# Gate projections by seven products ahead of the mLSTM, on normalised rows

## The chip, the cores and the metric

The kernel runs on one core of one Trainium2 chip. The metric is the device time of one execution in microseconds. Three runs of the kernel before gave 1904.54, 1907.61 and 1908.16 us: a median of 1907.61. The profile is one more execution, which took 1907.19 us.

## The reference

One layer of a hybrid encoder is applied to two request groups of 512 tokens each (x_prompt and x_sample, D = 1024), with shared weights:

```
u      = rmsnorm(x, g_mix) @ w_in       # one projection, its columns feed everything below
q, k   = silu(centred_conv(u[q,k], w))  # 4 heads of 128
v, o   = u[v], u[o]                     # 4 heads of 256 each; o gates the mLSTM's output
h      = mlstm(q, k, v, i, f), forward and backward, then a norm per head, times sigmoid(o)
a      = latent attention(cq, ckv, shared rotary key): 8 heads
y      = sigmoid(gm) * (h @ w_mo) + sigmoid(ga) * (a @ w_ao)
x      = x + y @ w_out
x      = x + swiglu(rmsnorm(x))         # the FFN
x      = x + gated embedding of p       # 256 -> 1024
out    = rmsnorm(x)
```

What matters here is that all columns of u come from the same normalised rows, and that o (8 blocks of 128 columns), gm and ga (8 blocks each) are plain 1024-to-128 projections, each behind a sigmoid.

## The kernel before

**Products.** Activations lie with features on the partitions and the 512 tokens of a group on the free axis. A product in fp32 is made of three matmuls of rounded parts, high by high, high by low and low by high. `proj1` (L173) does one block of 128 output columns for one group: 8 slices of the input times 3, so 24 matmuls of 128x512. `w8` (L186) loads a block of weights (512 KB) and splits it into `whi` (a cast on ScalarE) and `wlo` (a subtraction on VectorE).

**Seven products.** Some projections go by Strassen's scheme in Winograd's form. A quad is two output blocks by two input halves by two groups. `Ops` (L786) keeps the operands of the activation side: P1, P2 and P3 are plain quarters, P7, P6, P5 and Q4 are sums of them, and each is split into `xh` (ScalarE) and `xl` (VectorE). `Seven` (L847) loads four weight blocks, forms their sums on GpSimd and splits each into a high and a low half in one tile `wp` (L843 on ScalarE, L152 on VectorE); each product is 12 matmuls, so a quad takes 84 where eight products take 96. `chain` (L899) lets the products of neighbouring quads interleave, and `outputs` (L923) collects the banks: copies `u` on ScalarE, sums on VectorE. Before the change this serves the two branches' output projections ("mo", then "ao", whose operand sums are made by `oops`, L1013, on GpSimd except P7) and the FFN.

**The order of the work.** Everything below is told in the program's order; a scheduler moves instructions ahead where their inputs allow it.

- *Start.* x is loaded and multiplied by g_mix while it is split into `h` (pairs of high and low tiles of rows that are not yet normalised). `norm_x` (L292) squares x in place (six tiles on ScalarE, two on GpSimd), adds the squares (VectorE and GpSimd), and gets rstd per token from a matmul with ones (`sumsq`, into bank ssc) and one Newton sequence on VectorE (`rsqrt`). Since rows aren't normalised, each projection is multiplied by rstd on its way out of PSUM: `hproj` (L328) does it on VectorE for q, k, o and the merge gates; v has it as a scale. The latents (cq, ckv) and the mLSTM's gate logits are projected first.
- *Row computation.* The mLSTM's forget and input gates become cumulative rows on VectorE (L378 to L453, through two small transfers by way of DRAM); transposes on TensorE (`tpc`) turn them into columns `mcols`.
- *mLSTM.* `mlstm_proj(hd)` (L462) projects q, k, v and the two o blocks of a head. `mlstm_chain(hd, g)` (L531) does two passes for a group, one per direction: bc and bd (TensorE), exponentials into the tile `w` (ScalarE), a product with the scores (VectorE), `ph` (ScalarE) and `pl` (VectorE), then nm (TensorE, 128x258), the division and the norm, transposes `ht`, and `hz` (times the o gate). `w` has one buffer. The projections of head hd + 1 stand beside the chains of head hd.
- *The last head.* No projections are left for it. `lat_norms` (L608), which normalises the latents, stands ahead of the last head's chains, and ten merge gates (`merge_gate`, L642; `BULK[0] = 10`) beside them.
- *Attention*, with the other six merge gates between its heads, then the branches "mo" and "ao", the output projection, the embeddings (`emb`, L1102, whose weights sit in two of the tiles `wst` that `Seven` uses), the FFN, and the last norm.

Weights come by two queues, SP's and ScalarE's; SP's also carries stores of intermediate rows to DRAM (the merge gates to `tmd` and `tad`) and their loads.

## Time and profile before

| | |
|---|---|
| median of 3 runs | 1907.61 us (1904.54 to 1908.16) |
| the profiled execution | 1907.19 us, its span 1905.4 us |
| TensorE's granted clock, mean | 0.988 |
| busy: PE, DVE, ACT, POOL | 1849.6, 1242.5, 879.7, 477.5 us |
| DMA | 207.58 MB, mean 109 GB/s |

The profile's rows read as follows. In a timeline a row begins with its start and its duration in us, then engine, line, operation, result and inputs, tile sizes and a count; in brackets stands how long the engine had idled before, and what ended that. Matmuls overlap: one of 128x512 shows 0.39 us, but they start every 0.23 us, and it is the distance of starts that counts. In a table of stretches each engine has its busy time and, in brackets, its instructions; the number behind the engines is the clock that TensorE was granted, 1.00 being full. In a table of groups the time busy and the mean duration in ns stand behind the first bar, the idle time before such instructions behind the second. Stages by time in us, roughly: start 0 to 80, mLSTM heads 80 to 425, the last head's chains with ten merge gates 425 to 545, attention to 880, the branches to 1000, output projection and embeddings to 1150, the FFN to 1800, the end to 1905.

### The profile page before, as it was taken

The page shows a single profiled execution, that of the slowest core. Times are in us where ns is not written, and L with a number is a line of the kernel's source. Part 1 is how long each engine was busy: PE and PEld are TensorE (multiplying, and loading weights), DVE is VectorE, ACT ScalarE, POOL GpSimd, SP SyncE. Part 2 cuts the span into 40 slices and gives each one's busy share as a digit, 9 for nine tenths or more (in the row PEclk, how much of TensorE's full clock was granted, in tenths as well). Part 3 has the DMA queues.
Part 4 walks back from the last instruction along what each step waited for, and adds up shares of the span by engine and source line. Part 5 has one row for each costly group of instructions (what it writes and reads, how often), then busy time and mean ns, then how long its engine had stood idle before and what let it go on. Part 6 is the DMA issues. An engine that isn't in the chain of part 4 may idle for free.

```text
span 1905.4 us, 24519 instructions
## 1 busy us (share of the span) xinstructions
PE 1849.6 (97%) x8840; PEld 1538.6 (81%) x8840; DVE 1242.5 (65%) x2141; ACT 879.7 (46%) x1711; POOL 477.5 (25%) x346
## 2 busy tenths in 40 slices
PE   7999999999999999899989998999999999999997
PEld 6898998988888878677877886888888887888886
DVE  7657575836556567976897577444444558878757
ACT  5255555644444565784434354333333344434442
POOL 3000000100000000342550026666465652322100
PEclk9999999999999999999999998999999999999999
DMA  4111111122253123345455241233222346534242
GB/s 164 51 45 34 56 34 56 34 67 73 78 176 132 54 70 110 106 149 210 154 184 181 88 166 50 100 112 109 94 100 93 129 137 222 162 130 141 89 127 89
DMA packets 97881, 207.58 MB, mean 109 GB/s; under 512 B 10656, under 2 KB 21280, under 8 KB 97760
## 3 DMA queue, kind: packets, MB, share of 16 engines
q1 hardware_dynamic: 85664, 163.03, 25.5%
q10 hardware_dynamic: 12096, 43.00, 7.0%
q8 instruction: 69, 1.13, 0.2%
q14 instruction: 52, 0.43, 0.1%
HBM read 151.89 MB, written 54.10 MB: 108 GB/s over the span
## 4 chain that ended last, share of the span: by engine, by line
PE 85%; DVE 8%; issue 2%; ACT 2%; POOL 1%; DMA 1%; SPq 0%; DVEq 0%; ACTq 0%; POOLq 0%
PE b L894 12%; PE b L896 12%; PE b L895 12%; PE mm L183 8%; PE mm L181 8%; PE mm L182 8%; PE nm L580 3%; DVE xl L152 2%; PE mm L79 2%; PE mm L495 2%; PE mm L497 2%; PE mm L496 2%; PE pt L759 1%; DVE wp L152 1%; PE mm L1243 1%
## 5 line engine op out<-in xcount | busy, mean ns | idle before, releaser
L894 PE MATMUL b<-xh,wp 128*128 128x512 f32 x1148 | 444.1, 395 | 13.3 <-ACT wp L843 6.4
L895 PE MATMUL b<-xl,wp 128*128 128x512 f32 x1148 | 451.1, 393 | 4.9 <-DVE xl L152 4.9
L896 PE MATMUL b<-xh,wp 128*128 128x512 f32 x1148 | 447.2, 394 | 3.7 <-DVE wp L152 3.6
L843 ACT CAST wp<-wst 128x512 fp32r<-128x512 f32 (+1 forms) x271 | 164.7, 612 | 306.7 <-PE b L896 238.8
L152 DVE TENSOR_TENSOR wp<-wst,wp 128x512 fp32r<-128x512 f32 (+1 forms) x271 | 248.3, 918 | 76.7 <-ACT wp L843 76.1
L894 PEld LDWEIGHTS b<-xh,wp 128*128 128x128 f32 x1148 | 217.4, 189 | 66.4 <-ACT wp L843 8.8
L896 PEld LDWEIGHTS b<-xh,wp 128*128 128x128 f32 x1148 | 217.4, 189 | 53.5 <-DVE wp L152 6.0
L895 PEld LDWEIGHTS b<-xl,wp 128*128 128x128 f32 x1148 | 217.4, 189 | 52.1 <-DVE xl L152 5.3
L181 PE MATMUL mm<-hh,whi 128*128 128x512 f32 x592 | 233.7, 395 | 7.4 <-ACT whi L166 7.2
L183 PE MATMUL mm<-hh,wlo 128*128 128x512 f32 x592 | 233.1, 396 | 2.3 <-DVE wlo L152 2.2
L182 PE MATMUL mm<-hl,whi 128*128 128x512 f32 x592 | 233.4, 395 | 0.7 <-DVE hl L277 0.7
L869 POOL TENSOR_TENSOR s<-wst,wst 128x512 f32<-128x512 f32 (+1 forms) x42 | 75.6, 1800 | 432.8 <-DMA wst<-w 255.0
L934 DVE TENSOR_TENSOR u<-b,u 128x512 f32<-128x512 f32 x90 | 61.6, 689 | 141.4 <-PE b L896 85.3
L181 PEld LDWEIGHTS mm<-hh,whi 128*128 128x128 f32 x592 | 112.6, 190 | 31.2 <-ACT whi L166 7.2
L183 PEld LDWEIGHTS mm<-hh,wlo 128*128 128x128 f32 x592 | 112.4, 190 | 26.6 <-DVE wlo L152 3.4
L182 PEld LDWEIGHTS mm<-hl,whi 128*128 128x128 f32 x592 | 112.4, 190 | 24.5 <-DVE hl L277 1.3
L166 ACT CAST whi<-wst 128x1024 fp32r<-128x1024 f32 (+1 forms) x71 | 73.0, 1029 | 103.9 <-PE mm L182 63.4
L152 DVE TENSOR_TENSOR xl<-ld,xh 128x512 fp32r<-128x512 f32 x121 | 97.7, 837 | 11.6 <-ACT xh L1178 6.6
L152 DVE TENSOR_TENSOR wlo<-wst,whi 128x1024 fp32r<-128x1024 f32 (+1 forms) x71 | 86.7, 1221 | 25.1 <-ACT whi L166 24.8
L929 ACT COPY u<-b 128x512 f32<-128x512 f32 x90 | 50.9, 588 | 110.6 <-PE b L896 79.1
L152 POOL TENSOR_TENSOR vnl<-avt,vnh 128x512 fp32r<-128x512 f32 x16 | 21.4, 1337 | 283.6 <-ACT vnh L156 260.9
L495 PE MATMUL mm<-whi,hh 128*128 128x256 f32 x256 | 72.3, 283 | 0.2 <-DVE cu L329 0.2
(333 smaller groups left out, 3570.4 us busy)
## 6 DMA issues: line engine op xcount, KB each, us to landing
wst<-w SPq DMA_DIRECT2D x75, 512.0 KB
wst<-w ACTq DMA_DIRECT2D x60, 512.0 KB
ld<-actd SPq DMA_DIRECT2D x77, 256.0 KB
actd<-t SPq DMA_DIRECT2D x44, 256.0 KB
actd<-sg SPq DMA_DIRECT2D x33, 256.0 KB
x<-x SPq DMA_DIRECT2D x32, 256.0 KB
ld<-hzd SPq DMA_DIRECT2D x32, 256.0 KB
wst<-wd ACTq DMA_DIRECT2D x16, 512.0 KB
```

What stands on the lines that cost most here:

```text
L152: e.tensor_tensor(out=out, in0=src, in1=hi.bitcast(F32), op=ALU.subtract)
L166: S.copy(hi[:, :n], st[:, :n])
L181: E.matmul(bk, whi[:, c], hi, start=k == 0, stop=False)
L182: E.matmul(bk, whi[:, c], lo, start=False, stop=False)
L183: last_mm[0] = E.matmul(bk, wlo[:, c], hi, start=False, stop=k == nk - 1)
L495: E.matmul(out, hi[:, tb], whi[:, n], start=k == 0, stop=False)
L843: S.copy(hi, src)
L869: GP.tensor_tensor(out=src, in0=a11, in1=a21, op=ALU.add)
L894: E.matmul(bk, whi[:, c], hi, start=bool(first) and k == 0, stop=False, **sk)
L895: E.matmul(bk, whi[:, c], lo, start=False, stop=False, **sk)
L896: E.matmul(bk, wlo[:, c], hi, start=False, stop=k == self.kh - 1, **sk)
L934: V.tensor_tensor(out=t, in0=b, in1=t, op=ALU.add if name == "P2" else ALU.subtract)
```

## The change

The code of `Ops`, `Seven`, `chain` and `outputs` moves up unchanged but for a parameter that says where tiles lie. What it does:

- **Normalised rows.** x is no longer squared in place: ScalarE squares all tiles into other tiles, VectorE adds them in pairs, `sumsq` runs over four tiles of each group, rstd is spread by fp32 matmuls, and 16 VectorE instructions multiply x by g_mix and rstd in place.
- **Gates ahead.** On these rows 4 quads (the 8 o blocks) and 5 quads (10 of the 16 merge gate blocks) are done by seven products ahead of the mLSTM. Their tanh goes to DRAM (`tod`, `tmd`, `tad`), and the mLSTM loads its o gates from there. GpSimd makes their weight sums, VectorE their operand sums.
- **Behind that**, `h` is the normalised operands P1, P2, P3 and a split of the last quarter, so that q, k, v and the remaining merge gates need no multiplication by rstd: q and k are copied by ScalarE, the gates' tanh reads PSUM.
- **Pools.** The row computation's tiles are opened only once the chain's pools are closed, so it stands behind the chain.
- **The last head** has 2 merge gates beside it instead of 10; attention has 4 instead of 6.
- **Embeddings.** Their weights sit in four operand tiles of 128x512 instead of two of the `wst` tiles.
- **Second branch.** All operand sums of `oops` go to VectorE.

```diff
     def norm_x(g):
-        q = xs[g]
+        q = []
         for k in range(KD):
-            if k in (2, 5):
-                GP.tensor_tensor(out=q[k], in0=q[k], in1=q[k], op=ALU.mult)
-            else:
-                S.activation(out=q[k], in_=q[k], func=AF.Square)
-        for i, j, e in ((2, 5, GP), (0, 1, V), (3, 4, GP), (6, 7, V), (0, 3, V), (2, 6, V), (0, 2, V)):
-            e.tensor_tensor(out=q[i], in0=q[i], in1=q[j], op=ALU.add)
+            t = XT("t", "sq")
+            S.activation(out=t, in_=xs[g][k], func=AF.Square)
+            q.append(t)
+            if k % 2:
+                V.tensor_tensor(out=q[k - 1], in0=q[k - 1], in1=t, op=ALU.add)
+        pc = bank("ssc")
+        sumsq(pc, q[::2])
+        r = rsqrt(pc[:, 0 : 2 * NB], 2 * NB, 1.0 / D)
+        V.tensor_copy(out=rcol[g], in_=r)
+        bc = spread_f32(r)
         t = H("rs", "rs1")
-        S.copy(t, rstd_bank(q[:1], D, X0, rcol[g]))
+        S.copy(t, bc)
         rs1.append(t)
+        for k in range(KD):
+            x = xs[g][k]
+            V.scalar_tensor_tensor(out=x, in0=x, scalar=col("g_mix", k), in1=bc, op0=ALU.mult, op1=ALU.mult)
...
+    hx = Ops(lambda g, k: xs[g][k], lambda: XT("t", "t"), lambda n: V, place0)
+    hx.need("P7")
...
+    def first_pair(*cols_):
+        def put(at, t):
+            (kind, c), g = cols_[at[0]], at[1]
+            o = utile("o") if at == (0, 1) else t
+            S.activation(out=o, in_=t, func=AF.Tanh, scale=0.5)
+            if kind == "o":
+                S.activation(out=o, in_=o, func=AF.Identity, scale=hg[:, c : c + 1], bias=hg[:, c : c + 1])
+            nc.sync.dma_start(dsts[kind][g][c], o)
+
+        srcs = [a["w8"][W8[f"{kind}{c}"]] for kind, c in cols_]
+        return hx, lambda: Seven(srcs, 4, hx, outputs(put, utile))
...
+    quads = [first_pair(("o", 2 * i), ("o", 2 * i + 1)) for i in range(MH)]
+    quads += [first_pair(*bulk[2 * i : 2 * i + 2]) for i in range(FIRST)]
+    bulk = bulk[2 * FIRST :]
+    chain(quads, head=True)
...
+    h = [hx.x["P1"] + hx.x["P2"], bs + hx.x["P3"]]
+    WX.close()
+    XT.close()
+    MC = Slots("MC", sel=2)
+    R = Slots("R", "right", r=12, tr=2)
...
             for g in range(G):
-                bk = hproj(w, g, M1("tr", "cu"))
+                bk = M1("tr", "cu")
+                S.copy(bk, proj1(w, h[g]))
...
-        for c in range(2):
-            w = w8(f"o{2 * hd + c}")
-            for g in range(G):
-                to[g][c] = hproj(w, g, M1("to", "to"))
-                S.activation(out=to[g][c], in_=to[g][c], func=AF.Tanh, scale=0.5)
...
+        for g in range(G):
+            for c in range(2):
+                to[g][c] = M1("to", "to")
+                nc.sync.dma_start(to[g][c], tod[g][2 * hd + c])
...
             w = w8(f"{name}{c}")
             for g in range(G):
-            t = hproj(w, g, EV("bk", "tg"))
-            S.activation(out=t, in_=t, func=AF.Tanh, scale=0.5)
-            nc.sync.dma_start(dst[g][c], t)
...
+            t = EV("bk", "tg")
+            S.activation(out=t, in_=proj1(w, h[g]), func=AF.Tanh, scale=0.5)
+            nc.sync.dma_start(dsts[name][g][c], t)
...
-    oops = Ops(lambda g, k: load(ozd[g][k], X2, "x"), lambda: late["OP"]("ev", "t"), lambda n: V if n == "P7" else GP)
+    oops = Ops(lambda g, k: load(ozd[g][k], X2, "x"), lambda: late["OP"]("ev", "t"), lambda n: V)
...
-            st = [sl_("wst", "wst", F32, (P, 1024)) for sl_ in (WX, WX)]
-            for i in range(2):
-                nc.sync.dma_start(st[i], a["wple"][i])
+            st = [load(a["wple"][i // 2][:, i % 2 * T : i % 2 * T + T], OP, "ev") for i in range(4)]
...
-BULK = [10, 2, 1, 1, 0, 2, 0, 0, 0, 0]
+FIRST = 5
+BULK = [2, 1, 1, 1, 0, 1, 0, 0, 0, 0]
```

More of the change, by code (lines that the diff above doesn't have):

```diff
@@ L130, in bank @@
         return pb[0](n)
-    banks("P1", dict(mm=2, sc=2, tp=2, bc=2), mm="mm", sc="sT nm", tp="ssc tpc vtp ht", bc="bc bd rbc")
     cols = cp.tile([P, NCOL], F32, name="cols")
@@ new lines, in chain, with make @@
+    def chain(quads, head=False, look=4):
+        order = [(0, n) for n in ("P1", "P2", "P7")]
+        if head:
+            order = [(0, "P1"), (0, "P2"), (1, "P1"), (1, "P2"), (0, "P7"), (0, "P6"), (0, "P5"), (0, "Q4"), (1, "P7"), (0, "P3")]
+        for i in range(1 if head else 0, len(quads)):
+            for n in ("P6", "+P1", "P5", "+P2", "Q4", "+P7", "P3"):
+                if n[0] != "+":
+                    order.append((i, n))
+                elif i + 1 < len(quads):
+                    order.append((i + 1, n[1:]))
+        made = {}
+        def make(i):
+            if i not in made:
+                made[i] = quads[i][1]()
+        for at, (q, n) in enumerate(order):
+            for i, m in order[at : at + look + 1]:
+                quads[i][0].need(m)
+            for i, _ in order[at : at + 2]:
+                make(i)
+            made[q].product(n)
@@ L281, in encoder_kernel @@
     LAT = Slots("LAT", "right", raw=8)
     H = Slots("H", h=32, rs=2)
-    MC = Slots("MC", sel=2)
-    X0 = Slots("X0", x=16, raw=2, tr=15)
-    R = Slots("R", "right", r=12, tr=2)
+    XT = Slots("XT", x=16, t=28)
+    WX = Slots("WX", "right", wst=2, s3=2, wp=1)
+    banks("P0", dict(mm=4, tp=2, bc=2), mm="mm", tp="ssc", bc="rbc")
     h, rs1 = [], []
-    xs = [[X0("x", "x") for _ in range(KD)] for _ in range(G)]
+    xs = [[XT("x", "x") for _ in range(KD)] for _ in range(G)]
     def split_x(g):
@@ L316, in encoder_kernel @@
     split_x(0)
-    early["gate", 0] = raw(proj1(wg, h[0]), X0)
+    early["gate", 0] = raw(proj1(wg, h[0]), XT, "t")
     wq = w8("cq0")
```

313 lines of the change are left out of this document (153 added, 160 removed).

## The prediction

> **What bounds the kernel now.** I read the page first, then the busy time of each engine by stretches, then single rows. The page gives the span and TensorE's share.
>
> ```profile
> span 1905.4 us, 24519 instructions
> PE 1849.6 (97%) x8840; PEld 1538.6 (81%) x8840; DVE 1242.5 (65%) x2141; ACT 879.7 (46%) x1711; POOL 477.5 (25%) x346
> ```
>
> TensorE is busy for 97% of the span; its idle time is 1905.4 − 1849.6 = 55.8 us. So either its work must shrink or those 55.8 us must. The stretches (length, then busy time and count of PE, PEld, DVE, ACT and POOL, then the granted clock) say where it idles.
>
> ```profile
> 100.00:400.00 300.00, 300.00 (x1864) 270.81 (x1864) 192.30 (x431) 163.99 (x401) 15.86 (x26) 1.00 0.14 46
> 425.00:545.00 120.00, 120.00 (x590) 101.50 (x589) 70.15 (x173) 47.80 (x117) 1.50 (x3) 0.99 0.27 91
> 650.00:900.00 250.00, 238.47 (x1125) 192.75 (x1124) 186.08 (x372) 165.87 (x331) 55.78 (x40) 0.99 0.37 121
> 1200.00:1250.00 50.00, 50.00 (x220) 41.00 (x220) 22.15 (x28) 17.80 (x31) 32.37 (x22) 1.00 0.36 125
> ```
>
> From 100 to 400 (mLSTM heads) and 425 to 545 (the last head) TensorE never stops: VectorE's 64% and ScalarE's 55% are hidden there. Clean work runs at 50/220 = 0.2275 us for a 128x512 matmul. Two starts of product chains are holes:
>
> ```profile
> 950.00:970.00 20.00, 13.42 (x49) 10.24 (x48) 20.00 (x20) 6.45 (x12) 14.71 (x9) 0.83 0.62 198
> 1155.00:1175.00 20.00, 13.72 (x46) 10.24 (x45) 15.99 (x14) 7.08 (x12) 13.97 (x10) 0.74 0.19 66
> ```
>
> Twenty microseconds hold 88 matmuls; 49 and 46 were run. The first start loses 39 × 0.2275 = 8.9 us, the second 42 × 0.2275 = 9.6, part of it waiting, part of it at a lowered clock.
>
> **TensorE's work.** Eight o blocks and ten gm and ga blocks, two to a quad, now go by seven products: 84 matmuls for a quad where eight products took 96. Nine quads save 9 × 12 = 108, at 0.2275 us 24.6 us. Against that: sums of squares over four tiles instead of one for each group (32 matmuls for 8), and a spread of rstd by 128x128 matmuls in full fp32. Their rows count each such instruction twice:
>
> ```profile
> 29.45 0.95 PE L219 MATMUL ssc<-onesr,x 128*128 128x2 f32 x8
> 30.26 0.48 PE L182 MATMUL mm<-hl,whi 128*128 128x512 f32 x1
> ```
>
> ```profile
> 1087.97 1.05 PE L244 MATMUL rbc<-ident,rw 128*128 128x128 f32 x8
> 1088.78 0.48 PE L183 MATMUL mm<-yh,wlo 128*128 128x512 f32 x1
> ```
>
> Four sums took 30.26 − 29.45 = 0.81 us, 0.20 each; 24 more make +4.8. Four spreads took 0.81, so two groups +1.6, less the four 128x512 spreads that they replace (0.9): +0.7. Net **−19.1 us**, and all of it counts, since TensorE bounds these stages. The 64 multiplications by rstd leave VectorE, off this path.
>
> **The new chain's start.** The chain opens at a place where TensorE has never waited. On VectorE, just behind the second group's rstd, stood before the mLSTM's row computation:
>
> ```order
> L232 TENSOR_TENSOR diag_415<-ident,rl_409 128x512
> L338 TENSOR_TENSOR gsb_432<-raw_286,rs_78_382 128x512
> L152 TENSOR_TENSOR wlo_564<-wst_560,whi_562 128x1024
> L378 SCALAR_TENSOR_TENSOR u<-lf 128x64
> L388 TENSOR_SCALAR lf<-lf 128x64
> L380 TENSOR_SCALAR z<-u 128x64
> L381 RECIPROCAL z<-z 128x64
> ```
>
> Now stand there the operands' low halves (xl), their sums (t) and the weights' low halves (wp):
>
> ```order
> L465 COPY rcol_77<-rw_496 128x8
> L150 TENSOR_TENSOR xl_733<-x_95,xh_731 128x512
> L150 TENSOR_TENSOR xl_737<-x_96,xh_735 128x512
> ...
> L305 TENSOR_TENSOR t_703<-x_103,x_107 128x512
> L150 TENSOR_TENSOR wp_767<-wst_763,wp_767 128x512
> L150 TENSOR_TENSOR wp_809<-wst_763,wp_809 128x512
> L150 TENSOR_TENSOR xl_928<-x_107,xh_926 128x512
> L150 TENSOR_TENSOR xl_707<-t_703,xh_705 128x512
> L305 TENSOR_TENSOR t_709<-x_104,x_108 128x512
> ```
>
> The row computation is gone from here and some 70 operand steps came in, which must be done before TensorE has run out of the first eight products. What such steps cost beside GpSimd, whose weight sums start here too, the second start shows:
>
> ```profile
> 944.45 0.67 DVE L152 TENSOR_TENSOR wp<-wst,wp 128x512 fp32r<-128x512 f32 x1
> ...
> 956.87 1.76 DVE L152 TENSOR_TENSOR wp<-wst,wp 128x512 fp32r<-128x512 f32 x1
> ```
>
> ```profile
> 957.00 0.79 PE L895 MATMUL b<-xl,wp 128*128 128x512 f32 x1 [4.89 <-DVE xl L152]
> ...
> 961.42 0.39 PE L895 MATMUL b<-xl,wp 128*128 128x512 f32 x1
> ```
>
> 0.67 us alone, 1.76 beside GpSimd, and TensorE stood 4.89 us for an xl there. Before, VectorE had the second group's rstd at
>
> ```profile
> 42.94 0.17 DVE L255 COPY rcol<-rw 128x8 f32<-128x8 f32 x1
> ```
>
> 43 us; with eight multiplications of x more it is about 48 now. TensorE's ten projections (240 matmuls, 54.6 us) and sums end at about 73, so it has 25 us of them left, and 8 × 2.73 = 22 us of products. Seventy steps of 0.67 are 47 us, and ten slowed ones add 11: 47 + 11 − 25 − 22 = 11 late, somewhat less since the last steps aren't for the first eight. That is the size of the two old starts (8.9, 9.6): I take **+9** (4 to 14). Once running, the chain's 36 GpSimd sums (1.7 us each, 61) and its casts lie under 756 × 0.2275 = 172 us of products.
>
> **The mLSTM's start.** The row computation now begins behind the chain.
>
> ```profile
> 57.48 0.23 DVE L378 SCALAR_TENSOR_TENSOR u<-lf 128x64 f32<-128x64 f32 x1 [4.10 <-DMA lf<-rid]
> ...
> 95.53 0.28 DVE L453 COPY mcols<-tpc 128x32 f32<-128x32 f32 x2
> ```
>
> It ran 95.53 − 57.48 = 38 us, under projections. Its loads now stand on SP's queue behind the chain's last gate stores, so it can't begin sooner. Ahead of its transposes TensorE now has 96 q/k matmuls (21.8 us) and 84 of 256 columns for v, at about half, 10: **+6.5** (0 to 10). In heads 0 to 2 the o gates no longer fill. By its counts a head is o 96 × 0.2275 = 21.8 us, q and k 21.8, v 192 × 0.12 = 23, nm 14, the rest some 9: 90, and 68 without o. VectorE's 64% of 90 is 58, less eight multiplications of 0.69: 52, three quarters of 68. The nearest stage with such a mix is attention, 650 to 900, which idles 11.5 of 250, 4.6%; on 200 us that would be 9. I take **+5** (0 to 20).
>
> **The last head.** Here the change takes the cover away. TensorE's rows before, around the bc and bd of a pass (mm is a merge gate):
>
> ```order
> L181 MATMUL mm_4958<-hh_153,whi_4953 128x512
> L543 MATMUL bc_4401<-nmr,sel_4399 128x512
> L182 MATMUL mm_4958<-hl_155,whi_4953 128x512
> L183 MATMUL mm_4958<-hh_153,wlo_4955 128x512
> L181 MATMUL mm_4958<-hh_157,whi_4953 128x512
> ...
> L183 MATMUL mm_4987<-hh_229,wlo_4955 128x512
> L545 MATMUL bd_4403<-nmr,sel_4399 128x512
> L546 MATMUL bd_4403<-mask_633,identr 128x512
> L181 MATMUL mm_4987<-hh_233,whi_4953 128x512
> ```
>
> and now, behind the latents' sums of squares:
>
> ```order
> L181 MATMUL mm_5885<-xh_938,wlo_5854 128x512
> L236 MATMUL rbc_5341<-diag_5342,onesr 128x512
> ...
> L236 MATMUL rbc_5383<-diag_5387,onesr 128x512
> L757 MATMUL bc_5398<-nmr,sel_5396 128x512
> L759 MATMUL bd_5400<-nmr,sel_5396 128x512
> L760 MATMUL bd_5400<-mask_2110,identr 128x512
> L757 MATMUL bc_5474<-nmr,sel_5472 128x512
> L759 MATMUL bd_5476<-nmr,sel_5472 128x512
> L760 MATMUL bd_5476<-mask_2114,identr 128x512
> L794 MATMUL nm_5422<-va_5000,ph_5404 128x258
> ```
>
> Ten gates (480 matmuls) stood between; two are left, and they end before the spreads (rbc). From there to attention's first product only rbc, bc, bd, nm and ht remain. The steps that this uncovers, latent norms first, then a pass:
>
> ```profile
> 431.56 0.38 DVE L620 TENSOR_TENSOR ro<-ssc,rcol 128x8 f32<-128x8 f32 x4 [7.57 <-PE ssc L219]
> ...
> 451.16 1.40 DVE L629 SCALAR_TENSOR_TENSOR raw<-raw,cols,rbc 128x512 f32<-128x512 f32 x2
> ...
> 455.41 1.66 ACT L558 ACTIVATE w<-bc,mcols 128x128 f32<-128x128 f32 x6 [3.51 <-PE bc L543]
> 457.86 1.12 ACT L558 ACTIVATE w<-bd,mcols 128x128 f32<-128x128 f32 x4
> 458.24 1.70 DVE L566 TENSOR_TENSOR w<-w,st 128x512 f32<-128x512 f32 x4 [1.00 <-ACT w L558]
> 459.97 1.27 ACT L567 CAST ph<-w 128x1280 fp32r<-128x1280 f32 x1 [0.99 <-DVE w L566]
> 461.27 1.49 DVE L152 TENSOR_TENSOR pl<-w,ph 128x1280 fp32r<-128x1280 f32 x1 [1.33 <-ACT ph L567]
> ...
> 463.48 1.64 ACT L558 ACTIVATE w<-bc,mcols 128x128 f32<-128x128 f32 x6
> ```
>
> Norms: 431.56 to 452.47 is 20.9 us, less about 4.5 of gates' work between: 16. A pass is a chain, since its tile w is single: exponentials, mask product, ph, pl, from 455.41 to 462.76, 7.35 us; the next began 8.07 after it. Four passes at 7.2: 29. Then the last eviction, rstd, scaling, transposes, latents' casts:
>
> ```profile
> 525.06 0.17 ACT L582 ACTIVATE dn<-nm 128x1 f32<-128x1 f32 x1 [0.36 <-PE nm L580]
> ...
> 526.97 0.17 DVE L196 TENSOR_SCALAR rv<-ssm 128x4 f32<-128x4 f32 x1 [0.64 <-ACT nm L595]
> ...
> 529.98 1.14 DVE L598 TENSOR_SCALAR hm<-hm,rw 128x256 f32<-128x256 f32 x4
> ...
> 535.41 0.69 DVE L604 TENSOR_TENSOR hz<-to,ht 128x512 f32<-128x512 f32 x1
> ```
>
> About 2 + 2.4 + 1.1 + 0.9 + 2 = 8. In all 53 us. TensorE's work in them, with nm at
>
> ```profile
> 474.92 0.40 PE L580 MATMUL nm<-va,ph 128*128 128x258 f32 x2
> ...
> 475.27 0.41 PE L580 MATMUL nm<-va,ph 128*128 128x258 f32 x2
> ```
>
> 0.35/3 = 0.12 us: 120 nm 14.2, 30 gate matmuls left behind the last sum 6.8, 20 rbc, bc and bd 4.6, 16 ht 1.8: 27.4. Uncovered 53 − 27.4 = 25.6 us. After such idleness the clock is low: from 957.00 to 961.42 ten matmuls took 4.4 us instead of 2.3, so 2 more per long gap. The Trainium skill ("TensorE: Matmul & The Clock Gate", Part 1: the HAM clock gate) says that TensorE falls to half clock after an idle window of about 3.4 us and needs about 3.4 us of work to come back; by that a resumption costs 1.7 us, and the trace's 2.1 agrees. With one or two such ramps I take **+29** (17 to 36).
>
> **The second branch's sums** leave GpSimd:
>
> ```profile
> 936.40 6.39 POOL L808 TENSOR_TENSOR t<-t,ld 128x512 f32<-128x512 f32 x3 [5.57 <-DVE xl L152]
> ```
>
> ```profile
> 1138.78 16.70 POOL L869 TENSOR_TENSOR s<-wst,wst 128x512 f32<-128x512 f32 x1 [5.94 <-DMA wst<-w]
> ...
> 1160.53 6.28 POOL L814 TENSOR_TENSOR t<-t,hn 128x512 f32<-128x512 f32 x4
> ```
>
> On GpSimd such a sum takes 1.7 us, twelve of them 20; on VectorE 12 × 0.67 = 8, and its own steps stop being slowed (1.1 us each). **−4** (+3 to −8.9). The Trainium skill ("SBUF — State Buffer", Who interferes with whom) says that a VectorE instruction with two SBUF inputs and a GpSimd one that reads SBUF shut each other out; the 1.76 agrees.
>
> **The FFN's start.** TensorE waits there for a weight sum's cast, then for its low half:
>
> ```profile
> 1163.46 0.79 PE L894 MATMUL b<-xh,wp 128*128 128x512 f32 x1 [3.55 <-ACT wp L843]
> 1167.41 0.79 PE L896 MATMUL b<-xh,wp 128*128 128x512 f32 x1 [2.73 <-DVE wp L152]
> ```
>
> GpSimd stood from 1138.78 on a sum whose weights had not landed until about 1154, and the four operand sums (1160.53) came behind it. The embeddings' weights now free both tiles, so two of the loads are queued earlier, and what is late next is the operand sums themselves: the eight weight sums ahead of them stay, 8 × 1.7 = 13.6 us. **−5** (0 to −9.6). Squares off GpSimd at the kernel's start: −2 (0 to −3), out of 10 us that TensorE idles in the first 50.
>
> **Sum.** −19.1 + 9 + 6.5 + 5 + 29 − 4 − 5 − 2 = +19.4. The profiled execution took 1907.2 (span 1905.4), the median 1907.6, so the two stand for each other: 1907.2 + 19.4 = 1926.6, say 1927.
>
> **Rivals.** First, faster: the last head's steps are a matter of VectorE's busy time, not of a chain. Between 425 and 545 its 70.15 us include gate work:
>
> ```profile
> L329 DVE TENSOR_TENSOR tg<-rs,mm 128x512 f32<-128x512 f32 x17 | 11.6, 685 | 15.3 <-PE mm L183 15.1
> ...
> L152 DVE TENSOR_TENSOR wlo<-wst,whi 128x1024 fp32r<-128x1024 f32 x8 | 9.8, 1220 | 0.7 <-ACT whi L166 0.7
> ```
>
> 70.15 − 11.6 − 9.8 − 5 (attention's low halves) = 44 us; 44 − 27.4 = 17 uncovered. If both old starts close too (−18), the new start costs 4 and the mLSTM hides its rows: −19.1 + 4 + 17 − 18 = −16, 1891. It decides if passes follow each other under 4.5 us; for it speaks that ScalarE's and VectorE's steps of two passes could overlap, against it the 8.07 us between passes and the single w. Chance 0.20. Second, slower still: heads 0 to 2 lose 10% of 200 us, 20 instead of 5, 1942, as VectorE is three quarters full there; TensorE's filler of projections speaks against. 0.15. Third, no change: the last head costs 17 and the new start 4, with the rest as forecast: 1910; with a little more from the old starts it is 1907. 0.08. Fourth, that the change doesn't do what it says: the order shows 756 matmuls of the seven products ahead of the mLSTM, so it does. The forecast itself has 0.57.
>
> The range leaves 1 in 10 out on each side: from 1895, inside the first rival, to 1944, the second's. A measurement tells 0.2%, 3.8 us, from no change: faster 0.20, same 0.08, slower 0.72.
>
> **What would show it.** Right: in the changed profile TensorE idles 20 us or more between the last spread and attention's first product, with a low clock in pieces; the first weights' products of the new chain wait for xl; POOL's sums are gone around the second branch's start. Wrong: TensorE near 100% in the last head, passes 4.5 us apart, or the starts still losing 9 us each.

## The result, and the profile after

The changed kernel took 1964.98 us (median of 4 runs, 1962.42 to 1970.14), the kernel before beside it 1907.88 (1904.54 to 1909.80): a ratio of 1.0306, 95% interval 1.0290 to 1.0322. It is 57 us slower; forecast were 19, with a range that ended at 1944. The direction was right and the size was not. The profiled execution took 1964.93 us.

The page of the changed kernel, beginning and TensorE's share:

```profile
span 1963.1 us, 24780 instructions
PE 1861.5 (95%) x8792; PEld 1539.0 (78%) x8792; DVE 1273.9 (65%) x2215; ACT 935.2 (48%) x1835; POOL 522.9 (27%) x362
```

The span grew by 57.7 us. TensorE's idle time went from 55.8 to 101.6 us, and its busy time grew as well, by 11.9, although it has 112 matmuls of 128x512 less (108 of products, 4 of spreads): in many places it ran at a lowered clock, and a slow matmul counts as busy. So idle time alone doesn't tell where the time went. A comparison by stages does. The stages are cut at TensorE instructions that both programs have. First the kernel before, by groups (count, shortest, median and longest duration in ns, then start of the first and of the last):

```profile
L514 PE MATMUL sT<-qh,kh x32: 387/392/400, 109.7 to 411.0; 128*128 128x512 f32 x32
L516 PE MATMUL sT<-qh,kl x32: 387/396/397, 110.2 to 411.5; 128*128 128x512 f32 x32
...
L742 PE MATMUL sc<-knh,qnh x64: 389/394/628, 583.1 to 853.0; 128*128 128x512 f32 x64
...
L768 PE MATMUL av<-apl,vnh x64: 388/389/504, 622.3 to 864.0; 128*128 128x512 f32 x64
```

and the changed kernel; its first row is the chain, which begins at 79.4:

```profile
L394 PE MATMUL b<-xh,wp x1400: 387/389/632, 79.4 to 1856.5; 128*128 128x512 f32 x175
...
L731 PE MATMUL sT<-qh,kh x32: 387/397/498, 300.5 to 559.9; 128*128 128x512 f32 x32
L733 PE MATMUL sT<-qh,kl x32: 387/396/398, 301.4 to 560.4; 128*128 128x512 f32 x32
...
L953 PE MATMUL sc<-knh,qnh x64: 389/389/628, 664.9 to 915.1; 128*128 128x512 f32 x64
...
L979 PE MATMUL av<-apl,vnh x64: 389/389/628, 702.1 to 927.4; 128*128 128x512 f32 x64
```

The first sT is head 0's, the last sT is head 3's, the first sc begins attention, the last av ends it. For each stage, TensorE's instructions in the program's order times their steady pitch (0.2275 us for 128x512, 0.12 for 256 or 258 columns, 0.11 for the transposes, 0.20 for a sum of squares) give the work; the rest of the stage is loss, by waiting or by clock. (A spread of rstd in fp32 takes 0.20 us by its rows and stands here at 0.11; that puts 0.7 us of the changed kernel's start under loss which are work.)

```
stage (us)                     before: length  work  loss   changed: length  work  loss   loss added  forecast
start to first sT                      109.7   93.4  16.3            300.5  268.1  32.4      +16.1     +13.5
heads (first to last sT)               301.8  301.1   0.7            259.9  236.4  23.5      +22.8      +5
last head (to first sc)                171.6  169.3   2.3            104.5   61.3  43.2      +40.9     +29
attention (to last av)                 280.9  260.4  20.5            262.5  238.6  23.9       +3.4       0
branches, FFN, end                    1041.4  986.3  55.1           1035.7  986.3  49.4       -5.7      -9
sum                                   1905.4 1810.5  94.9           1963.1 1790.7 172.4      +77.5     +38.5
```

The work fell by 19.8 us, and the losses grew by 77.5: that is the 57.7. Two of the five stages hold 64 of the 77.5, the heads and the last head. The windows of these two in the changed kernel:

```profile
300.00:560.00 260.00, 244.58 (x1566) 221.09 (x1565) 167.13 (x408) 146.64 (x385) 13.35 (x27) 0.97 0.17 56
560.00:665.00 105.00, 79.36 (x353) 62.50 (x352) 67.67 (x172) 50.20 (x127) 1.87 (x3) 0.82 0.26 88
```

Both stages were at 100% before. In the second the granted clock is 0.82.

### The profile page after: what moved, and what is told of

Its sections match the earlier page's. It is cut to its first block, busy times and chain, and to the rows that moved or that the text cites. A ratio compares the mean times of both kernels' runs of the same rounds, so it can differ in the third digit from the quotient of the medians.

```text
span 1963.1 us, 24780 instructions
## 1 busy us (share of the span) xinstructions
PE 1861.5 (95%) x8792; PEld 1539.0 (78%) x8792; DVE 1273.9 (65%) x2215; ACT 935.2 (48%) x1835; POOL 522.9 (27%) x362
## 4 chain that ended last, share of the span: by engine, by line
PE 80%; DVE 11%; ACT 4%; DMA 2%; issue 2%; POOL 1%; SPq 0%; DVEq 0%; ACTq 0%
PE b L394 15%; PE b L396 14%; PE b L395 14%; PE mm L179 4%; PE mm L181 4%; PE mm L180 4%; PE nm L794 3%; PE mm L79 2%; DVE xl L150 2%; PE mm L715 2%; PE mm L716 2%; PE mm L717 1%; DVE wp L150 1%; PE mm L1291 1%; PE mm L1290 1%
## 5 line engine op out<-in xcount | busy, mean ns | idle before, releaser
L394 PE MATMUL b<-xh,wp 128*128 128x512 f32 x1400 | 541.7, 395 | 11.9 <-ACT u L429 6.3
L396 PE MATMUL b<-xh,wp 128*128 128x512 f32 x1400 | 545.3, 394 | 7.5 <-DVE wp L150 7.5
L395 PE MATMUL b<-xl,wp 128*128 128x512 f32 x1400 | 549.2, 393 | 2.8 <-DVE xl L150 2.8
L394 PEld LDWEIGHTS b<-xh,wp 128*128 128x128 f32 x1400 | 264.8, 189 | 78.1 <-ACT u L429 11.9
L396 PEld LDWEIGHTS b<-xh,wp 128*128 128x128 f32 x1400 | 264.9, 189 | 67.6 <-DVE wp L150 9.8
L395 PEld LDWEIGHTS b<-xl,wp 128*128 128x128 f32 x1400 | 264.7, 189 | 61.3 <-DVE xl L150 4.6
L372 POOL TENSOR_TENSOR wst<-wst,wst 128x512 f32<-128x512 f32 (+1 forms) x51 | 104.5, 2049 | 56.7 <-DVE wp L150 53.2
L179 PE MATMUL mm<-xh,whi 128*128 128x512 f32 x224 | 87.9, 393 | 0.3 <-DVE va L150 0.3
L180 PE MATMUL mm<-xl,whi 128*128 128x512 f32 x224 | 87.4, 390 | 0.0
L181 PE MATMUL mm<-xh,wlo 128*128 128x512 f32 x224 | 86.8, 391 | 0.0
L379 POOL TENSOR_TENSOR wst<-wst 128x512 f32<-128x512 f32 (+1 forms) x51 | 73.4, 1441 | 44.6 <-DVE wp L150 42.4
L370 POOL TENSOR_TENSOR wst<-wst 128x512 f32<-128x512 f32 (+1 forms) x51 | 81.1, 1589 | 3.8
L715 PE MATMUL mm<-whi,xh 128*128 128x256 f32 x256 | 74.9, 293 | 6.1 <-DVE va L150 3.4
```

Source lines behind the costliest of these rows:

```text
L179: E.matmul(bk, whi[:, c], hi, start=k == 0, stop=False)
L180: E.matmul(bk, whi[:, c], lo, start=False, stop=False)
L181: last_mm[0] = E.matmul(bk, wlo[:, c], hi, start=False, stop=k == nk - 1)
L370: GP.tensor_tensor(out=a21, in0=a21, in1=a22, op=ALU.add)
L372: GP.tensor_tensor(out=a11, in0=a11, in1=a21, op=ALU.add)
L394: E.matmul(bk, whi[:, c], hi, start=bool(first) and k == 0, stop=False, **sk)
```

## The experiments

All times are medians, each beside the kernel before on the same chip (1906.8 to 1909.1). The losses by stage, worked out as above from each run's own profile and its own order, stand here for all experiments on the changed kernel; the text below uses them.

```
loss by stage (us)      start  heads  last head  attention  rest   gate blocks beside the last head
before                   16.3    0.7      2.3      20.5     55.1   10
changed                  32.4   23.5     43.2      23.9     49.4    2
e1_back                  29.8   22.1      9.3      26.6     46.7   10
e2_spread                32.4    5.0     26.4      22.6     48.5    4, and 6 behind the heads' projections
e3_norms                 34.7   39.8     25.4      22.1     46.8    2
e4_banks                 36.3   27.1     29.1      23.1     48.7    2
e5_ohome                 30.9    1.1     21.6      24.2     52.3    6, and the o gates in the heads
e6_w2                    30.4   18.6     44.0      23.3     50.6    2
e7_cu                    31.7   27.7     44.1      25.1     47.4    2
```

The last head's loss splits at the first of attention's products (632.59 in the changed kernel). Ahead of it lies the chain from the last sum of squares on: latent norms, four passes, divisions. Behind it lie attention's first products, some 114 matmuls, up to the first sc. By the same counting:

```
loss (us)                    before  changed  e1_back  e2_spread  e3_norms  e4_banks  e5_ohome  e6_w2  e7_cu
chain                           0.4     36.7      0.5       19.2      18.9      25.0      11.9   37.6   35.9
attention's first products      0.1      6.3      8.6        7.0       6.5       2.2       7.8    6.3    6.4
```

**Eight gate blocks back beside the last head.**

```diff
-FIRST = 5
-BULK = [2, 1, 1, 1, 0, 1, 0, 0, 0, 0]
+FIRST = 1
+BULK = [10, 1, 1, 1, 0, 1, 0, 0, 0, 0]
```

> Eight merge gate blocks leave the chain ahead of the mLSTM (four quads less) and stand beside the last head again, ten in all. TensorE gets 48 matmuls more, 10.9 us. Theory (the last head's steps lost their cover; by the stages of the changed profile that costs 41 us): 1965 + 11 - 41 = 1935, between 1928 and 1942, and TensorE near 100% in the last head. Rival (the gates beside it were no cover; the time went to the lower clock and to the work that was added ahead of the mLSTM): 1965 + 11 = 1976, with idle stretches in the last head as before.

Measured: 1939.1 us (ratio 1.0168, 1.0145 to 1.0190), inside the theory's range. The windows of the heads and of the last head in this kernel:

```profile
221.00:480.00 259.00, 245.51 (x1567) 222.19 (x1566) 168.61 (x410) 146.97 (x386) 13.26 (x27) 0.97 0.17 57
480.00:638.00 158.00, 152.79 (x735) 128.07 (x734) 76.60 (x179) 66.62 (x150) 1.86 (x3) 0.98 0.32 112
```

The last head's loss fell from 43.2 to 9.3 us, for 10.9 us of matmuls more; the heads kept theirs (22.1). With ten blocks the chain itself loses 0.5 us: the gates beside the last head were its cover, and taking them away cost more than seven products save on them. The other 8.6 us are not the chain's. TensorE waits there, among attention's first products, for ScalarE's copies of av:

```profile
PE mm L887 <- ACT av L891: 5.2, 2, 5.0
```

In ScalarE's queue these copies stand behind casts of the rotary key (kh, at 603.23 and 611.29), which wait for VectorE. In the kernel before, those casts (547.13 and 553.58) came while gates still ran, up to 557. Why they come later here no run shows.

**The same work, with six of the ten blocks behind the heads' projections.**

```diff
         if hd < MH - 1:
             mlstm_proj(hd + 1)
+            for _ in range(2):
+                merge_gate(*bulk.pop(0))
...
+FIRST = 1
+BULK = [4, 1, 1, 1, 0, 1, 0, 0, 0, 0]
```

> The same work for TensorE as in e1_back, but of the ten gate blocks six stand behind the projections of heads 1 to 3 and four beside the last head. Theory (heads 0 to 2 lose some 25 us because the o gates no longer fill TensorE's waits for the chains): 18 to 20 of the 25 come back, and the last head, with 44 us of cover for some 41, loses 5 to 10 again: 1920 to 1930. Rival (the heads lose time because copies of q and k went to ScalarE's queue or because rows and o gates arrive late; filler doesn't help): the heads keep their 25, the last head loses 5 to 10: 1940 to 1946.

Measured: 1937.8 us (1.0144, 1.0124 to 1.0163), no different from e1_back, and between the ranges of theory and rival.

```profile
224.00:511.00 287.00, 284.00 (x1761) 254.75 (x1760) 174.07 (x415) 157.26 (x399) 14.19 (x27) 1.00 0.20 66
511.00:640.00 129.00, 113.00 (x535) 93.83 (x535) 70.18 (x174) 55.55 (x135) 1.86 (x3) 0.93 0.31 103
```

In the heads the theory held: 284 of 287 us busy, a loss of 5.0 instead of 22.1, so that 17 us came back, close to the forecast 18 to 20. In the last head the forecast was too small: four blocks there leave 26.4 us of loss, 19.2 of them in the chain, where 5 to 10 were expected. The cover only moved, and what the heads gained the last head lost.

**The o gates back in the heads**, three quads of merge gates ahead of the mLSTM.

```diff
-    quads = [first_pair(("o", 2 * i), ("o", 2 * i + 1)) for i in range(MH)]
-    quads += [first_pair(*bulk[2 * i : 2 * i + 2]) for i in range(FIRST)]
+    quads = [first_pair(*bulk[2 * i : 2 * i + 2]) for i in range(FIRST)]
...
-        for g in range(G):
-            for c in range(2):
+        for c in range(2):
+            w = w8(f"o{2 * hd + c}")
+            for g in range(G):
                 to[g][c] = M1("to", "to")
-                nc.sync.dma_start(to[g][c], tod[g][2 * hd + c])
+                S.activation(out=to[g][c], in_=proj1(w, h[g]), func=AF.Tanh, scale=0.5)
...
+FIRST = 3
+BULK = [6, 1, 1, 1, 0, 1, 0, 0, 0, 0]
```

> Changed kernel with the o gates back in the heads' projections (on the normalised rows, so still without a multiplication by rstd), three quads of merge gates ahead of the mLSTM, six merge gates beside the last head and four in attention. Against the kernel before TensorE has 36 matmuls less (-8.2) and the sums and spreads more (+5.5), the chain's start costs 9.5, the mLSTM's start 3, attention 3, the branches give 5. Theory (the heads' loss is the missing o gates): heads as before, the last head loses 0 to 6, 1914 to 1922. Rival (the heads lose to ScalarE's copies and the late rows, not to missing cover): some 20 more, 1934 to 1942.

Measured: 1931.6 us (1.0138, 1.0121 to 1.0155); the profile is of the slowest of its executions, 1939.1.

```profile
184.00:490.00 306.00, 305.84 (x1863) 273.66 (x1862) 177.82 (x417) 172.60 (x420) 14.65 (x27) 1.00 0.15 47
490.00:637.00 147.00, 136.38 (x636) 113.04 (x635) 74.48 (x178) 63.50 (x146) 1.86 (x3) 0.93 0.29 101
```

The heads are at 305.84 of 306 us, a loss of 1.1: their 23 us were the missing o gates. ScalarE's copies of q and k and the row computation behind the chain are as in the changed kernel, and once the gates fill, they cost nothing there. The whole came out 10 us above the theory and just under the rival's range, since the last head with six blocks still loses 21.6 and not 0 to 6. Over these runs the chain's loss falls with the blocks beside it, 36.7 with two, 19.2 with four, 11.9 with six, 0.5 with ten, by less than the 10.9 us of work that a block has. With four and six blocks their matmuls run out before the chain does: the last one starts at 572.8 in e2_spread and at 581.7 in e5_ohome, and the last division's square ends at 602.6 and 597.0. In e1_back gates run until 603. The loss in attention's first products doesn't fall with the blocks (6.3 to 8.6).

**Latent norms one head earlier.**

```diff
-LATN = (3, 0)
+LATN = (2, 0)
```

> Changed kernel with the latents' norms one head earlier, ahead of head 2's chains. Theory (the 16 us from the last sum of squares to the first pass are part of the last head's uncovered chain): about 14 us less, 1951, between 1947 and 1956. Rival (head 2 has no cover to spare either, so they cost there what they save): 1963 to 1967.

Measured: 1960.8 us (1.0267, 1.0250 to 1.0284), 4 less than the changed kernel, outside both ranges, nearer to the rival's. The last head lost 17.8 us less, as much as the norms take, and the heads 16.3 more. The 16 us are part of the uncovered chain, but head 2 has no cover to spare either.

**Four banks for the last head's nm.**

```diff
-                bk = bank("nm")[:, 0:258]
+                bk = bank("mm" if hd == MH - 1 and i % 2 else "nm")[:, 0:258]
```

> Changed kernel in which every second nm of the last head uses a bank of the projections' pair, so that four banks instead of two serve its divisions. Theory (what the prediction missed in the last head are the evictions, 15 us from the last pass's low half to the last division where one eviction of 2 us was counted, since each nm waits for a bank to be read out): 6 to 9 us less, 1956 to 1959. Rival (the passes set the pace and the evictions only fill what they leave, with the low clock making nm slow): within 2 of 1965.

Measured: 1954.2 us (1.0236, 1.0219 to 1.0253), 10.8 less than the changed kernel, more than the theory's 6 to 9. Heads and last head together lose 56.2 us instead of 66.7. The fourth pass's ph and the last square of the divisions (ScalarE's accumulator reads), in this kernel:

```profile
600.13 1.26 ACT L781 CAST ph<-w 128x1280 fp32r<-128x1280 f32 x1 [0.58 <-DVE w L780]
...
608.45 0.19 ACT L809 ACTIVATION_READ_ACCUMULATOR mm<-hm 128x1 f32 x1
```

From the cast's start to the end of the last square it takes 8.5 us; in the changed kernel, whose rows follow below, 18.2. No gate runs in that stretch of the changed kernel, and here the first starts only a microsecond before its end, at 607.38, so this is the divisions' own gain. But the edit did a second thing: nm now takes banks of the merge gates' pair, and the two gate blocks, which ran from 544.7 to 575.1 in the changed kernel, run here behind the divisions, from 607.4 to 630.0. There they cover the scaling, the transposes and the casts, and attention's first products lose 2.2 us instead of 6.3; the heads lose 27.1 instead of 23.5. How much of the 10.8 us is the banks' and how much the gates' place isn't separated.

**Two buffers for w.**

```diff
-    MC = Slots("MC", sel=2)
+    MC = Slots("MC", sel=1)
...
-    M1 = Slots("M1", qk=8, tr=4, to=4, va=4, S=8)
+    M1 = Slots("M1", qk=8, tr=4, to=2, va=4, S=8)
...
-    M2 = Slots("M2", w=1, ph=2, pl=2, hm=2)
+    M2 = Slots("M2", w=2, ph=2, pl=2, hm=2)
```

> Changed kernel with two buffers for the passes' tile w; for space the o gates' tiles are two instead of four and sel one instead of two. Theory (the single w makes a pass wait for the one before it, 6.4 us from pass to pass in the changed profile): passes come 4.5 to 5.5 us apart, the last head's loss of 43 falls by 5 to 8 and the heads' 23 by up to 5: 1952 to 1960. Rival (the evictions with their two banks set the end, and passes that come sooner only wait there): within 2 of 1965.

Measured: 1952.7 us (1.0232, 1.0217 to 1.0247), 12 less; its profile is of the slowest execution (1959.4) and shows only 5.5 of the 12. In that profile the four casts to ph of the last head:

```profile
581.58 1.32 ACT L781 CAST ph<-w 128x1280 fp32r<-128x1280 f32 x1
...
587.09 1.33 ACT L781 CAST ph<-w 128x1280 fp32r<-128x1280 f32 x1
...
595.15 1.26 ACT L781 CAST ph<-w 128x1280 fp32r<-128x1280 f32 x1 [0.49 <-PE nm L794]
...
603.85 1.24 ACT L781 CAST ph<-w 128x1280 fp32r<-128x1280 f32 x1
```

They come 5.5, 8.1 and 8.7 us apart; the changed kernel's came 6.3, 6.0 and 8.9 apart. The last head's loss is the same (44.0), the heads' fell by 4.9. So the time lies in the theory's range, but not where the theory put it: in this profile the single w costs something in the heads and doesn't set the last head's end, and there the rival holds. Where the rest of the 12 us lies its profile doesn't show.

**The copies of q and k on VectorE.**

```diff
-                S.copy(bk, proj1(w, h[g]))
+                V.tensor_copy(out=bk, in_=proj1(w, h[g]))
```

> Changed kernel with the copies of q and k on VectorE instead of ScalarE. Theory (the heads' loss is missing filler, not ScalarE's queue): within 3 of 1965. Rival (ScalarE's queue holds the exponentials): the heads lose 8 to 15 less, 1950 to 1957.

Measured: 1965.9 us (1.0303, 1.0288 to 1.0318), as the changed kernel: the theory. Taking the copies out of ScalarE's queue gains nothing in the heads (27.7 us of loss). Since they went to VectorE's queue, which the chains use as well, a gain there that is lost again here isn't excluded by this run; that the copies cost nothing once the heads are filled is shown by e5_ohome.

**The parts that aim at later stages, alone on the kernel before.** First the second branch's sums:

```diff
-    oops = Ops(..., lambda n: V if n == "P7" else GP)
+    oops = Ops(..., lambda n: V)
```

> The kernel before with only the second branch's operand sums moved to VectorE. Theory (as predicted: TensorE's wait at that start is VectorE slowed beside GpSimd): -4, between -3 and -6, so 1903 to 1906. Rival (the twelve sums only lengthen VectorE's queue and the start costs as much): -1 to +3.

Measured: 1900.3 us beside 1906.8 (0.9971, 0.9959 to 0.9982), 5.5 us faster by the ratio, inside the theory's 3 to 6 (6.5 by the medians). The window around that start, in the kernel before and in this one:

```profile
945.00:970.00 25.00, 18.42 (x71) 14.38 (x70) 25.00 (x23) 8.89 (x17) 19.71 (x12) 0.86 0.57 179
1150.00:1175.00 25.00, 18.72 (x68) 14.38 (x67) 20.99 (x23) 10.44 (x17) 18.97 (x10) 0.80 0.16 53
```

```profile
945.00:970.00 25.00, 22.62 (x98) 17.72 (x96) 25.00 (x38) 11.24 (x20) 13.24 (x4) 1.00 0.72 226
```

98 matmuls instead of 71 in 25 us, at the full clock.

Then the embeddings' weights:

```diff
-            st = [sl_("wst", "wst", F32, (P, 1024)) for sl_ in (WX, WX)]
-            for i in range(2):
-                nc.sync.dma_start(st[i], a["wple"][i])
+            st = [load(a["wple"][i // 2][:, i % 2 * T : i % 2 * T + T], OP, "ev") for i in range(4)]
...
```

> The kernel before with only the embeddings' weights in operand tiles. As predicted (weights that land late hold GpSimd and with it the FFN's first sums): -5, 1904. Rival (VectorE's steps slowed beside GpSimd's four operand sums are what comes last there; in the changed profile TensorE still waited 5.35 us for a weight's low half): within 1 of the kernel before.

Measured: 1905.3 us (0.9987, 0.9978 to 0.9997), 2.5 us by the ratio (0.6 to 4.2 by the interval): less than the prediction's 5; the rival's 1 is not excluded. With both parts (f1_oops_wple, below) the FFN's start, in the same window as the last row of the kernel before, gains only 5 matmuls:

```profile
1150.00:1175.00 25.00, 19.48 (x73) 15.20 (x72) 14.76 (x15) 7.98 (x14) 13.27 (x9) 0.86 0.15 52
```

The second branch's and the FFN's operand sums together on VectorE, without the embeddings' edit, add this to the first:

```diff
-    h2 = Ops(hn, lambda: OP("ev", "t"), lambda n: GP if n == "Q4" else V)
+    h2 = Ops(hn, lambda: OP("ev", "t"), lambda n: V)
```

> The kernel before with the second branch's and the FFN's operand sums all on VectorE. Theory (both starts lose their time to VectorE steps that take 1.7 us beside GpSimd instead of 0.67): -4 and again -4 to -7, so 1897 to 1901. Rival (the FFN's start is held by the weights' arrival): as p1_oops, 1903 to 1906.

Measured: 1900.2 us (0.9960, 0.9947 to 0.9974): in the theory's range, but no different from p1_oops, since the intervals overlap.

```profile
1100.00:1150.00 50.00, 46.75 (x206) 38.42 (x205) 41.00 (x62) 26.69 (x48) 12.27 (x8) 0.97 0.37 127
1150.00:1175.00 25.00, 23.92 (x105) 19.38 (x105) 18.38 (x30) 13.11 (x23) 12.81 (x5) 1.00 0.15 53
```

At the FFN's start 105 matmuls ran instead of 68, 8.4 us; but, against the branch's sums alone, 206 instead of 224 in the 50 us ahead and 87 instead of 98 around the second branch's start, which together give 6.6 back. The start's own theory held, and the whole did not move.

The first two edits together:

> The kernel before with two of the change's parts, the second branch's sums on VectorE (alone 1900.3 beside 1906.8) and the embeddings' weights in operand tiles (alone 1905.3). Theory (they act at different starts and add up): -6.5 - 1.5, 1898 to 1900. Rival (the second only moves with noise): as the first alone, 1900 to 1902.

Measured: 1899.2 us beside 1908.1 (0.9955, 0.9942 to 0.9968): the theory's range. The interval overlaps that of p1_oops, so the second part's share isn't shown by it.

All three edits together:

> As f1_oops_wple, and the FFN's operand sums all on VectorE too. With the sums alone the FFN's start gained 37 matmuls (8.4 us) and 18 were lost in the 50 us ahead of it, with a wait of 3.3 us for an embedding's copy. Theory (GpSimd's and VectorE's queues ahead of that start are eased by the earlier weight loads, so that part of the 8.4 stays): 1893 to 1897. Rival (what VectorE takes over there is given back in the embeddings whatever the loads do): 1898 to 1900.

Measured: 1895.6 us beside 1908.1 (0.9935, 0.9919 to 0.9950): the theory's range, and the fastest of all, 0.65% below the kernel before and 3.5% below the changed one. Its interval overlaps that of f1_oops_wple, so the last 3.6 us between these two stay open.

## Why the prediction was wrong, by its steps

**TensorE's work (−19.1)** was right: −19.8 by the counts of both programs, −19.1 with the spreads at their 0.20.

**The new chain's start (+9)** was right: from 79.4 to the first q product at 261.2 the changed kernel took 181.8 us for 756 × 0.2275 = 172.0; with five quads (e1_back) the same excess was 9.6. The size is partly luck. TensorE did wait for an xl, as forecast, but only for 2.8 us; banks that ScalarE copies took 2.2 more, and the rest is a lowered clock and short delays. Of the other terms there, the squares' −2 did not come (16.6 us are lost ahead of the chain, where the kernel before lost 16.3 up to its first sT), and the mLSTM's start, forecast at 6.5, lost 4.8 between 261.2 and the first sT. The whole stretch to the first sT lost 16.1 more than before, where the prediction's three terms there (9, 6.5 and −2) make 13.5.

**Heads 0 to 2 (+5, 0 to 20)** failed: 22.8. The step that failed took VectorE's share, three quarters, and attention's idle 4.6% for the measure. What counts is a few places in TensorE's order where the chains' steps and the read-outs that stand in line with them aren't done and no independent product is left to run. TensorE's waits in the changed kernel's heads (total us, times, longest):

```profile
PE bc L757 <- ACT w L772: 5.4, 2, 4.6
PE mm L715 <- DVE va L150: 3.4, 1, 3.4
```

and one such place, the end of head 1's chains, where the next head's projections had run out; 9.3 us are lost there, between 430 and 450:

```profile
436.71 0.50 PE L794 MATMUL nm<-va,ph 128*128 128x258 f32 x2 [0.95 <-ACT nm L809]
...
442.85 0.77 PE L757 MATMUL bc<-nmr,sel 128*128 128x512 f32 x1 [4.61 <-ACT w L772]
```

TensorE waits 0.95 us for a bank that ScalarE still reads, and 4.61 us with bc for exponentials; the clock falls, and the next matmuls are slow as well. Another 6.8 us are lost between 510 and 530, and there projections were left: at 520.97 a product of v waits 3.35 us for a bank whose read-out on VectorE (va) stands behind a pass's pl. Shares of busy time can't show this: VectorE was at 167.13 of 260 us. That the o gates were this cover is shown by e5_ohome (1.1) and, with other gates in their place, by e2_spread (5.0).

**The last head (+29, 17 to 36)** had the right mechanism and a term too small: 40.9. The prediction counted the latent norms (16), four passes (29) and one last division with what follows (8). The exponentials of the four passes and the last ph in the changed kernel:

```profile
584.26 1.66 ACT L772 ACTIVATE w<-bc,mcols 128x128 f32<-128x128 f32 x6 [7.39 <-PE bc L757]
...
591.01 0.37 ACT L772 ACTIVATE w<-bd,mcols 128x128 f32<-128x128 f32 x1 [1.62 <-DVE pl L150]
...
597.34 0.37 ACT L772 ACTIVATE w<-bd,mcols 128x128 f32<-128x128 f32 x1 [0.88 <-DVE pl L150]
...
603.35 0.37 ACT L772 ACTIVATE w<-bd,mcols 128x128 f32<-128x128 f32 x1 [0.88 <-DVE pl L150]
...
609.33 1.26 ACT L781 CAST ph<-w 128x1280 fp32r<-128x1280 f32 x1 [0.25 <-PE nm L794]
```

Norms were right: from the last sum at 568.6 to 584.26 it is 15.6. Passes were shorter than forecast, 6.4 apart. But the fourth ph came only at 609.33, behind a division in ScalarE's queue, and after it stood this, the first and the last of the remaining divisions on VectorE, and the scaling:

```profile
612.69 0.48 DVE L805 SCALAR_TENSOR_TENSOR hm<-nm,rc,hm 128x256 f32<-128x256 f32 x1
...
626.44 0.48 DVE L805 SCALAR_TENSOR_TENSOR hm<-nm,rc,hm 128x256 f32<-128x256 f32 x1
...
629.55 1.14 DVE L812 TENSOR_SCALAR hm<-hm,rw 128x256 f32<-128x256 f32 x4
```

Nine divisions were left for 612 to 627, each with nm, a bank to be read out, and the next nm behind it. The step that failed counted one of 2 us. Then the end:

```profile
629.96 1.97 PE L816 MATMUL ht<-ident,hm 128*128 128x128 f32 x8 [4.47 <-DVE hm L812]
...
632.59 1.30 PE L887 MATMUL mm<-whi,ckvh 128*128 128x512 f32 x2 [0.66 <-ACT cqh L154]
```

From 568.6 to 632.59 it is 64 us instead of 53. The norms took 15.6 (16 forecast), the passes with the late ph 27.8 up to the end of the fourth pl at 612.1 (29 forecast), and what follows 20.5 where 8 were forecast: the miss in the chain is this last term. That banks set its pace is shown by the stretch from the fourth ph to the last square in e4_banks, 8.5 us instead of 18.2. A second term was put at nothing: attention's first products, behind the chain, lose 6.3 us instead of 0.1, for ScalarE's copies of av and at a lowered clock, in e1_back as well, where the chain is covered; no run was aimed at it. The third thing that was too small is the clock. The prediction allowed for one or two ramps of 2 us; the windows (TensorE's busy time and count first, the granted clock third from the end) say

```profile
575.00:580.00 5.00, 2.45 (x9) 1.21 (x7) 4.32 (x8) 1.54 (x2) 0.00 (x0) 1.00 0.14 52
580.00:585.00 5.00, 2.05 (x4) 0.92 (x5) 4.69 (x7) 0.74 (x3) 0.00 (x0) 0.69 0.31 105
585.00:590.00 5.00, 3.53 (x7) 1.58 (x8) 2.27 (x5) 3.32 (x9) 0.58 (x2) 0.50 0.00 0
...
595.00:600.00 5.00, 4.02 (x22) 3.85 (x22) 2.89 (x4) 4.12 (x14) 0.00 (x0) 0.60 0.00 2
...
610.00:615.00 5.00, 2.68 (x10) 2.38 (x11) 3.54 (x13) 2.19 (x8) 0.00 (x0) 0.50 0.01 3
615.00:620.00 5.00, 5.00 (x27) 5.00 (x27) 2.55 (x14) 1.47 (x5) 0.00 (x0) 0.55 0.00 0
```

and nm ran at

```profile
613.93 0.42 PE L794 MATMUL nm<-va,pl 128*128 128x258 f32 x1
...
614.57 0.42 PE L794 MATMUL nm<-va,pl 128*128 128x258 f32 x1
```

0.64/3 = 0.21 us instead of 0.12. What the clock alone cost isn't separated by any run. The sign that the prediction named for being right, 20 us of idling or more and a low clock in pieces, came: TensorE idled 19.5 us between the last spread (its end at 581.48) and attention's first product, and the clock was low in pieces.

**The second branch's sums (−4, +3 to −8.9)** were right: −5.5 alone. The row of 0.67 us that the prediction calls alone (944.45) began just as GpSimd's next sum did; at 931.35, before GpSimd's sums, which begin at 936.40, the same step took 0.69, so the contrast with 1.76 stands.

**The FFN's start (−5)** was too large: −2.5 alone, with 0.6 to 4.2 by the interval. The step that failed took GpSimd's sum of 16.70 us at 1138.78 for a wait for weights. With the embeddings' weights out of the way such a sum is as long in the changed kernel,

```profile
1198.35 15.53 POOL L372 TENSOR_TENSOR wst<-wst,wst 128x512 f32<-128x512 f32 x1 [7.11 <-DVE wp L150]
```

and it took 15.53 us in p2_wple too. In all these traces VectorE runs steps one every 0.60 us through the whole of it, and the sum ends 1.2 us after the first step that reads a bank (u<-b,u: at 1154.25 in the kernel before, where the sum ends at 1155.48; at 1212.65 in the changed one, where it ends at 1213.88). So by the rows GpSimd was held by VectorE; no run tested it by itself. Behind it came GpSimd's operand sums, and in the changed kernel TensorE waited for a weight's low half,

```profile
1224.59 0.79 PE L396 MATMUL b<-xh,wp 128*128 128x512 f32 x1 [5.35 <-DVE wp L150]
```

since VectorE's steps beside these operand sums took 1.77 us instead of the 0.68 that they took while GpSimd was held:

```profile
1210.84 0.68 DVE L150 TENSOR_TENSOR wp<-wst,wp 128x512 fp32r<-128x512 f32 x1
...
1217.76 1.77 DVE L150 TENSOR_TENSOR wp<-wst,wp 128x512 fp32r<-128x512 f32 x1
```

With these sums on VectorE (p3_sums) the start nearly closed, 105 matmuls of some 110 that fit.

**The rivals.** The first, that VectorE's busy time alone sets the last head, is out: passes came 6.4 apart and the loss was 43. The second, slower still by the heads, came nearest; it and the forecast's last head were both true and more, so that the sum lay outside a range that took them as alternatives. The third, no change, is out. Of the 38 us by which the forecast missed, 17.8 lie in the heads and 11.9 in the last head.

## What to carry to other kernels

Work that an engine does beside a latency-bound chain is paid for already: before moving it to a cheaper form elsewhere, count the chain's steps with every division and buffer it waits for, at the clock that a half-idle TensorE gets, and ask what will stand in its place. A plain product that hides a wait can be worth more than the eighth that a seven-product scheme saves on it. Parts of a change that act in different stages are worth timing alone: here two of them alone bring the kernel from 1908.1 to 1899.2, a third of the same kind perhaps to 1895.6, while the change as a whole, with the gates ahead of the mLSTM as its largest part, stands at 1965.0.

## What the runs showed of the hardware

The clock fell without a long idle gap. Ahead of the first window at 0.50 TensorE's gaps were under 2 us,

```profile
577.85 1.10 PE L236 MATMUL rbc<-diag,onesr 128*128 128x512 f32 x2 [1.41 <-DVE raw L843]
...
583.43 0.79 PE L757 MATMUL bc<-nmr,sel 128*128 128x512 f32 x1 [1.95 <-DVE raw L843]
```

but it was busy for only 4.5 of the 10 us from 575 to 585. By the shares above it fell at about 582 (0.69 from 580 to 585) and came back at about 599 (0.60 from 595 to 600): 17 us at half, in which TensorE was busy for 11.2, where a start that ran densely had it back after 4.4 us (957.00 to 961.42 before). The Trainium skill ("TensorE: Matmul & The Clock Gate", Part 1: the HAM clock gate) tells of an idle window of about 3.4 us and of as much sustained work to come back; the dense start is compatible with the second, and the passes show that here several short gaps were followed by half clock as well, and that work with gaps in it didn't bring the clock back in that time.

VectorE and GpSimd held each other up in both directions. VectorE's step of 0.68 us took 1.77 beside GpSimd's sums, and a GpSimd sum, 1.63 us at 1213.96, took 15.53 at 1198.35, beside VectorE steps that followed each other every 0.60 us.
